# One row load of 128 partitions dealt as 120 and 8 partitions in a DMA-bound RMSNorm-and-repeat kernel

## The chip, the cores and the metric

The kernel runs on one core of one Trainium2 chip. The metric is the device time of an execution in microseconds (us). The two versions are compared by runs that alternate on the same chip.

## The reference

```python
def reference(x, gamma):                       # x: 8 x 512 x 2048 float32, gamma: 2048
    x_rep = np.repeat(x, 2, axis=1)            # each row twice
    rms = np.sqrt((x_rep ** 2).mean(axis=-1, keepdims=True) + 1e-6)
    return ((x_rep / rms) * gamma[None, None, :]).astype(np.float32)
```

33.6 MB are read and 67.1 MB are written, as the output has each row twice.

## The kernel before

The 4096 input rows are cut into 8 tiles. A tile has 128 partitions with K = 4 rows each. The SBUF tile `y` has 8 row slots for a partition: the four input rows are loaded into the upper four slots, and the results are written over the slots from below. There are three such buffers.

```python
    K = 4
    x_t = x.rearrange("b s d -> (b s) d").rearrange("(n p k) d -> n p k d", p=P, k=K)
    rows = ctx.enter_context(tc.tile_pool(name="rows", bufs=3))
    # ... other pools cut

    def load(i, parts=1):
        y = rows.tile([P, K * R, D], f32, name="y")
        step = K // parts
        for k in range(0, K, step):
            at = K * (R - 1) + k
            nc.sync.dma_start(out=y[:, at : at + step, :], in_=x_t[i, :, k : k + step, :])
        ys.append(y)

    load(0, parts=K)          # tile 0 row by row: four DMAs of 1 MB
    # ... gamma: one row from the ScalarE queue, then broadcast by GpSimd; eps by VectorE
    load(1)                   # 4 MB each
    load(2)
    for i in range(ntiles):
        for k in range(K):    # ScalarE: square with sum, sqrt; VectorE: reciprocal, x * rstd * gamma; one copy
            ...
        nc.sync.dma_start(out=out_t[i], in_=y.rearrange("p j d -> p (j d)"))   # 8 MB
        if i >= 1 and i + 2 < ntiles:
            load(i + 2)
```

Below, rows 0 to 3 are the four row loads of tile 0; the second and the third load are those of tiles 1 and 2.

Of the kernel before, what the change touches and what calls it, by code (L numbers as in the profile page):

```python
# [1 line left out]

# [4 lines left out]


@with_exitstack
def kernel(  # L10
    ctx: ExitStack,
    tc: tile.TileContext,
    x: bass.AP,
    gamma: bass.AP,
    out: bass.AP,
):
    nc = tc.nc
    P = nc.NUM_PARTITIONS
    f32 = mybir.dt.float32
    Act = mybir.ActivationFunctionType  # L20
    Alu = mybir.AluOpType

    B, S, D = x.shape
    Bo, So, Do = out.shape
    R = So // S
    assert R == 2 and D == Do and B == Bo and So == S * R
    eps = 1e-6
    inv_d = 1.0 / float(D)


    K = 4
    N = B * S
    assert N % (P * K) == 0
    ntiles = N // (P * K)
    x_t = x.rearrange("b s d -> (b s) d").rearrange("(n p k) d -> n p k d", p=P, k=K)
    out_t = out.rearrange("b s d -> (b s) d").rearrange("(n p j) d -> n p (j d)", p=P, j=K * R)

    singles = ctx.enter_context(tc.tile_pool(name="singles", bufs=1))
    rows = ctx.enter_context(tc.tile_pool(name="rows", bufs=3))
    junk = ctx.enter_context(tc.tile_pool(name="junk", bufs=1, space=bass.MemoryType.PSUM))  # L40
    small = ctx.enter_context(tc.tile_pool(name="small", bufs=8))

    ys = []

    def load(i, parts=1):


        y = rows.tile([P, K * R, D], f32, name="y")
        step = K // parts
        for k in range(0, K, step):  # L50
            at = K * (R - 1) + k
            nc.sync.dma_start(out=y[:, at : at + step, :], in_=x_t[i, :, k : k + step, :])  # L52
        ys.append(y)

    load(0, parts=K)
    gamma_b = singles.tile([P, D], f32, name="gamma_b")
    nc.scalar.dma_start(out=gamma_b[0:1, :], in_=gamma.partition_broadcast(1))
    nc.gpsimd.partition_broadcast(out_ap=gamma_b[:], in_ap=gamma_b[0:1, :])  # L58
    eps_t = singles.tile([P, 1], f32, name="eps_t")
    nc.vector.memset(eps_t, eps)  # L60
    load(1)
    load(2)

    for i in range(ntiles):
        y = ys[i]
        for k in range(K):
            xk = y[:, K * (R - 1) + k, :]
            y0, y1 = y[:, R * k, :], y[:, R * k + 1, :]
            sq = junk.tile([P, D], f32, name="sq")
            ss = small.tile([P, 1], f32, name="ss")  # L70
            nc.scalar.activation(out=sq[:], in_=xk, func=Act.Square, accum_out=ss[:])  # L71
            rms = small.tile([P, 1], f32, name="rms")
            nc.scalar.activation(out=rms[:], in_=ss[:], func=Act.Sqrt, scale=inv_d, bias=eps_t[:])  # L73
            rstd = small.tile([P, 1], f32, name="rstd")
            nc.vector.reciprocal(out=rstd[:], in_=rms[:])  # L75
            nc.vector.scalar_tensor_tensor(  # L76
                out=y0, in0=xk, scalar=rstd[:], in1=gamma_b[:],
                op0=Alu.mult, op1=Alu.mult,
            )
            if k == K - 1:  # L80
                nc.vector.tensor_copy(out=y1, in_=y0)  # L81
            else:
                nc.scalar.copy(out=y1, in_=y0)  # L83
        nc.sync.dma_start(out=out_t[i], in_=y.rearrange("p j d -> p (j d)"))  # L84
        if i >= 1 and i + 2 < ntiles:
            load(i + 2)


# [1 line left out]
_INS = ['x', 'gamma']  # L90
_OUTS = [((8, 1024, 2048), 'float32')]


# [23 lines left out]
```

## Time and profile before

| | before |
|---|---|
| time, median of 3 runs | 240.11 us (239.83 to 241.21) |
| span of the profiled run | 239.1 us |
| bytes moved, mean rate | 100.69 MB, 421 GB/s |
| VectorE, ScalarE busy | 37%, 49% |

All large DMAs are issued by SyncE and work through one queue in order: it has 100.66 of the 100.69 MB. The page's list of DMA issues gives the count, the KB of one and the median time from issue to landing:

```profile
y<-in_x_dram SPq DMA_DIRECT2D x7, 4096.0 KB, 38.8
y<-in_x_dram SPq DMA_DIRECT2D x4, 1024.0 KB, 8.0
out_dram<-y SPq DMA_DIRECT2D x8, 32.0
```

A 4 MB load takes 38.8 us to land although its data need 9.7 us (8 packets of 1.213 us on each engine). The rest is time behind other DMAs in the same queue.

DVE is VectorE, ACT is ScalarE, and SPq is SyncE issuing DMAs.

Two further readings come from the trace's records of DMA. A **landing mark** is the update of a DMA's semaphore by one of the engines; a DMA over all 16 engines has 16, as each 128-partition load of the kernel before shows. A **packet** is one partition's part of a DMA (8 KB in a row load, 32 KB in a tile's load, 64 KB in a store), with start and duration.

### The profile page before, as it was taken

What the parts mean: (1) busy time and instruction counts of PE and PEld (TensorE: products, weight loads), DVE (VectorE), ACT (ScalarE), POOL (GpSimd) and SP (SyncE); (2) the same over time, 40 slices, a digit from 0 to 9 for tenths busy, and PEclk for the clock granted to TensorE, in tenths of its full rate; (3) what the DMA queues carried; (4) which work ended last, traced back from release to release, by engine and by line L of the source; (5) the groups of instructions that cost most, each with busy time, mean ns of one, the idle gap of its engine ahead of it and who ended that gap; (6) DMA issues with size and microseconds to landing.
All of it is one profiled execution on the core that took longest, in us unless ns stands there. A gap on an engine that the chain in (4) does not pass through costs nothing.

```text
span 239.1 us, 293 instructions
## 1 busy us (share of the span) xinstructions
DVE 88.8 (37%) x73; ACT 116.3 (49%) x122; POOL 2.5 (1%) x5
## 2 busy tenths in 40 slices
DVE  0449759590000085400863016820168202591000
ACT  2998999950000299104990059800598006970000
POOL 4000000000000000000000000000000000000000
DMA  7999998989899999899898999899989899898984
GB/s 262 426 454 439 439 439 351 526 351 526 351 428 439 493 395 451 384 411 510 362 515 351 439 439 506 373 422 433 493 384 471 362 461 461 384 482 384 493 384 175
DMA packets 2741, 100.69 MB, mean 421 GB/s; under 512 B 306, under 2 KB 306, under 8 KB 306
## 3 DMA queue, kind: packets, MB, share of 16 engines
q1 hardware_dynamic: 2736, 100.66, 98.3%
q14 instruction: 3, 0.02, 0.0%
q10 hardware_dynamic: 2, 0.01, 0.0%
HBM read 33.56 MB, written 67.11 MB: 421 GB/s over the span
## 4 chain that ended last, share of the span: by engine, by line
DMA 68%; ACT 13%; DVE 8%; SPq 1%; issue 1%
DMA y<-in_x_dram 41%; DMA out_dram<-y 27%; ACT sq L71 7%; DVE y L76 6%; ACT y L83 5%; DVE y L81 2%; SPq L52 1%; ACT rms L73 1%; DVE rstd L75 0%; SPq L84 0%
## 5 line engine op out<-in xcount | busy, mean ns | idle before, releaser
L71 ACT ACTIVATE sq<-y 128x2048 f32<-128x2048 f32 x32 | 59.7, 1865 | 92.5 <-DMA y<-in_x_dram 92.5
L76 DVE SCALAR_TENSOR_TENSOR y<-y,rstd,gamma_b 128x2048 f32<-128x2048 f32 x32 | 75.3, 2352 | 1.2
L75 DVE RECIPROCAL rstd<-rms 128x1 f32<-128x1 f32 x32 | 5.1, 159 | 124.8 <-ACT rms L73 124.8
L83 ACT COPY y<-y 128x2048 f32<-128x2048 f32 x24 | 44.7, 1890 | 3.2 <-DVE y L76 3.2
L81 DVE COPY y<-y 128x2048 f32<-128x2048 f32 x8 | 9.8, 1226 | 0.3
L73 ACT ACTIVATE rms<-ss,eps_t 128x1 f32<-128x1 f32 x32 | 9.4, 293 | 0.7
L71 ACT ACTIVATION_READ_ACCUMULATOR sq<-y 128x1 f32 x32 | 6.0, 186 | 0.0
L58 POOL PARTITION_BROADCAST gamma_b<-gamma_b x1 | 2.3, 2293 | 2.1 <-DMA gamma_b<-in_gamma_dram 2.1
L71 ACT ACT_TABLE_LOAD x1 | 1.3, 1283 | 1.3 <-PEq L101 1.3
L73 ACT ACT_TABLE_LOAD x1 | 1.3, 1283 | 0.0
L60 DVE MEMSET eps_t<- 128x1 f32 x1 | 0.1, 59 | 0.8 <-PEq L101 0.8
L101 POOL MEMSET const-bfloat16-1.0<- 128x1 bf16 x1 | 0.1, 101 | 0.0
L101 POOL MEMSET const-uint8-127<- 128x1 uint8 x1 | 0.1, 101 | 0.0
L101 POOL MEMSET const-float32-0.0<- 128x1 f32 x1 | 0.1, 98 | 0.2 <-issue 0.2
L101 POOL MEMSET const-float32-1.0<- 128x1 f32 x1 | 0.1, 99 | 0.0
## 6 DMA issues: line engine op xcount, KB each, us to landing
y<-in_x_dram SPq DMA_DIRECT2D x7, 4096.0 KB, 38.8
y<-in_x_dram SPq DMA_DIRECT2D x4, 1024.0 KB, 8.0
out_dram<-y SPq DMA_DIRECT2D x8, 32.0
gamma_b<-in_gamma_dram ACTq DMA_DIRECT2D x1, 8.0 KB
```

The lines of the kernel that those rows point to most:

```text
L52: nc.sync.dma_start(out=y[:, at : at + step, :], in_=x_t[i, :, k : k + step, :])
L58: nc.gpsimd.partition_broadcast(out_ap=gamma_b[:], in_ap=gamma_b[0:1, :])
L60: nc.vector.memset(eps_t, eps)
L71: nc.scalar.activation(out=sq[:], in_=xk, func=Act.Square, accum_out=ss[:])
L73: nc.scalar.activation(out=rms[:], in_=ss[:], func=Act.Sqrt, scale=inv_d, bias=eps_t[:])
L75: nc.vector.reciprocal(out=rstd[:], in_=rms[:])
L76: nc.vector.scalar_tensor_tensor(out=y0, in0=xk, scalar=rstd[:], in1=gamma_b[:], op0=Alu.mult, op1=Alu.mult,)
L81: nc.vector.tensor_copy(out=y1, in_=y0)
L83: nc.scalar.copy(out=y1, in_=y0)
L101: nc = _bacc.Bacc("TRN2", target_bir_lowering=False, num_devices=1)
```

## The change

Row 0 of tile 0 is loaded by two DMAs, of partitions 0 to 119 and 120 to 127. If the DMA of 120 rows goes over 15 engines with 8 rows each, and that of 8 rows over eight, the intent is plain: take 8 rows off one engine and give one more to each of eight others, if that one engine is what ends late.

```diff
-            nc.sync.dma_start(out=y[:, at : at + step, :], in_=x_t[i, :, k : k + step, :])
+
+            cuts = (0, 120, P) if i == 0 and k < 1 else (0, P)
+            for p0, p1 in zip(cuts, cuts[1:]):
+                nc.sync.dma_start(out=y[p0:p1, at : at + step, :], in_=x_t[i, p0:p1, k : k + step, :])
```

All later lines of the kernel move down by three: the square is line 74, the load line 55, the store line 87.

## The prediction

The prediction numbers the 16 engines as names, since no trace numbers them: "15" is the one that the 120 rows leave out, "0 to 7" are those of the 8 rows. Before the run this deal was the author's estimate. So is rival 1: the packets of the two DMAs take longer, those of the 120 rows up to twice 309 ns, those of the 8 rows four times. No trace of the kernel before shows these factors.

> **What bounds the kernel now.** I read the page first: the slices, the queue table and the chain.
>
> ```profile
> DVE  0449759590000085400863016820168202591000
> ACT  2998999950000299104990059800598006970000
> ...
> DMA  7999998989899999899898999899989899898984
> ...
> q1 hardware_dynamic: 2736, 100.66, 98.3%
> ...
> DMA 68%; ACT 13%; DVE 8%; SPq 1%; issue 1%
> ```
>
> The DMA row is at 8 or 9 from the second slice to the last but one, while VectorE and ScalarE have whole slices of zero. All 100.66 MB go over one queue, whose packets fill 98.3% of the time of 16 DMA engines. The kernel is bound by its bytes. I checked that by a sum. The packets in the trace have three sizes with steady durations: 8 KB in 309 ns, 32 KB in 1213 ns, 64 KB in 2418 ns (medians). One engine of 16 carries 4 x 8 rows of 8 KB, 7 x 8 of 32 KB and 8 x 8 of 64 KB: 32 x 0.309 + 56 x 1.213 + 64 x 2.418 = 9.9 + 67.9 + 154.8 = 232.6 us. The first packet starts at 1.73 us, so an engine without a hitch would end at 234.3; the last packet ends at 237.66. Only some 3 us are slack or stalls.
>
> Second, the timeline of the SyncE queue and of the start, to see whether a queue ever runs dry.
>
> ```profile
> 0.72 3.20 SPq L52 DMA_DIRECT2D y<-in_x_dram  x6
> 24.12 15.65 SPq L84 DMA_DIRECT2D out_dram<-y  x2
> ...
> 5.67 1.88 ACT L71 ACTIVATE sq<-y 128x2048 f32<-128x2048 f32 x1 [3.11 <-DMA y<-in_x_dram]
> ```
>
> Six loads are issued in the first 3.9 us. ScalarE starts on row 0 of tile 0 at 5.67, when it lands, and tile 0's store is issued at 24.12. The third tile's load lands at 33.4, so the first store waits 8 to 9 us in the queue behind loads. A late first row costs compute time that is hidden. Line 71 of the kernel is the square, line 52 the load, line 84 the store.
>
> Third, the chain of waits at the end, the one place where compute comes close.
>
> ```profile
> 159.68 39.68 DMA y<-in_x_dram
> 199.36 0.02 issue
> 199.38 2.01 ACT sq L71 x2
> ...
> 212.30 2.36 DVE y L76
> 214.66 0.02 issue
> 214.68 1.23 DVE y L81
> ```
>
> The last load lands at 199.36, compute ends at 215.9, the last store is issued at 215.97. The engines leave the store before it between 216.80 and 218.69. An issue takes about 1.0 us to its first packet (issue 0.72, packet 1.73), so the quick engines wait a moment and the slow ones do not.
>
> Fourth, the landing marks. The trace has, for each 128-partition DMA, 16 marks, one per DMA engine, in order of time. Those of the first row run from 5.06 to 5.64 us; those of the last load from 197.49 to 199.36, eleven within 0.35 us and the last two at 199.32 and 199.36; those of the last store at 236.53 to 236.66 (eleven), then 236.96, 237.08, 237.27, 237.95, 237.99. So **two** engines run last, 0.04 us apart and 1.3 to 1.4 us behind the body, and the end is theirs. Linking each packet to the one that starts as it ends gives the same: the two were 0.3 us behind the median early and lost about 1.1 us more in the loads after 100 us.
>
> [...]
>
> **The change part by part.**
> - Issues: one more DMA on SyncE. Row loads take 0.38 to 0.66 us to issue there, so the second row's is about 0.45 us later (1.16 to about 1.6). The rows' data take 2.47 us each (8 x 0.309), so the queues stay ahead: hidden. No instruction of another engine is added; the order shows ScalarE waiting for one more semaphore before its first square.
> - Engine 15: 8 packets of 8 KB fewer, 8 x 0.309 = -2.47 us of work. It also starts only at the third issue, two issues later (about 0.9 us), so it runs about 1.6 us ahead.
> - Engines 0 to 7: one packet more, +0.31 us each. Engines 8 to 14: nothing. The bytes are the same: 8 x 15 + 8 = 128 rows.
> - First square: it now waits for engines 0 to 7's ninth packet, 5.67 + 0.31 = about 6.0 us. Hidden, with 8 us to spare.
> - The end: since engines are busy to the end, a shift at the start stays. [...] If the late pair is 15 and one of 8 to 14, the end stays at 237.95. If neither is 15, 0 to +0.3. Relieving one of two tied engines gains 0.04 us at most.
>
> Sum without further effects: 240.11 + 0 to 0.3 = about 240.1 to 240.4.
>
> **The rivals.**
> 1. [...] each packet up to twice as long, +2.47 us for the row; [...] 4 x 0.309 = 1.24 us in place of 0.31. Together up to 3.7 us on engines 0 to 7, which stays to the end: up to 243.8. For it: 64 KB in 2.42 us, 27 GB/s, looks like a hard limit[...]. Against it: the first row is already spread by latency (first packets of 0.47 to 1.33 us against 0.309 later), so part of a conflict hides. I give it a bit under one half, with half its full size as the likely value.
> 2. **A gain at the tail.** The two late engines lose time together, in the same loads, as if they share something. If relieving 15 relieves both, the last load lands up to 1.6 us earlier, the last store is issued earlier and the end falls to about 236.5: up to -1.4 us, 238.7. It can't be more: the body of the engines ends at 236.5. I give it one in six.
> 3. **A new wait in compute**, the first row landing later and pulling the first store late. It needs more than 8 us at the start; even rival 1 gives below 4. Nothing.
> 4. **ScalarE or VectorE as the bound**: 116.3 and 88.8 us busy of 239.1. Nothing.
>
> **Range and chances.** Weights: unchanged to +0.4 us, about 0.4; contention of +0.5 to +3.7 us, 0.42; gain of up to 1.4 us, 0.16. The runs of the kernel before already spread from 239.83 to 241.21. I put the middle at **240.5 us** and the range at 239.2 to 243.2. Faster by over 2% would need 4.8 us, more than the 3 us or so that are slack, so 0.01; slower by over 2% needs +4.8 us, more than the full contention[...]: 0.04. Within 2%: 0.95.
>
> **What the profile after would show.** Right: the DMA with 120 partitions has 15 late marks and one early, that with 8 partitions 8 late ones; the second and later rows' marks show one engine about 1.6 us ahead of the others; the first square starts near 6.0; the queue stays at 98%; the last store still has at least one engine 1.3 us behind the body. Rival 1: the first row's packets longer than 309 ns after the first ones, the square starting at 7 us or later, and every later landing late by as much. Rival 2: the last store's 16 marks within 0.7 us. The prediction is wrong if 120 partitions go to fewer than 15 engines (8 engines with 15 rows each would cost 7 x 0.309 = 2.2 us at once)[...].

## More of the kernel before

The view by windows gives the stretch, its length, the busy us (and instructions) of VectorE, ScalarE and GpSimd, and the granted clock. The last two numbers are the share of the 16 DMA engines' time and GB/s, counted from the packets that start in the stretch, so a share can be over 1.

```profile
3.00:13.00 10.00, 3.56 (x4) 6.82 (x8) 1.85 (x1) 1.00 1.05 442
5.00:7.00 2.00, 0.00 (x0) 1.33 (x1) 0.00 (x0) 1.00 1.04 438
```

The four row loads run at full rate from 3 us on, as fast as later stretches (442 GB/s here, 439 from 13 to 33 us).

## The result, and the profile after

| | before | after |
|---|---|---|
| median | 240.17 us (239.83 to 241.21, 4 runs) | 243.35 us (242.31 to 243.69, 4 runs) |
| ratio | | 1.0118, 95% interval 1.0073 to 1.0163 |

A ratio here is the mean time of one kernel's fast runs over the mean of the other's of the same rounds, so it is not quite the ratio of the medians. The changed kernel is **1.2% slower**, some 2.8 us. By the 2% line this still counts as the same.

Lines of the page of the kernel after, the slices of DMA and the queue:

```profile
DMA  7999999898989998999898999899989898988984
...
q1 hardware_dynamic: 2743, 100.66, 97.9%
```

These hardly tell the two apart. The engines count as busy all the time; the bytes are the same; seven packets are new, which are semaphore marks (the queue has 311 packets of 4 bytes in place of 304). The loss is visible only where busy engines move less. The same windows as before, of the kernel after:

```profile
3.00:13.00 10.00, 0.00 (x0) 3.87 (x4) 1.96 (x1) 1.00 1.00 303
5.00:7.00 2.00, 0.00 (x0) 0.00 (x0) 0.00 (x0) 1.00 1.13 209
```

From 5 to 7 us the engines were as busy as before and moved 209 GB/s in place of 438: half. Nearly every 8 KB packet that started between 3.5 and 6.5 us took about 520 to 650 ns, where before it took 309.

SyncE's queue and ScalarE's start, from the timeline of the kernel after:

```profile
0.72 4.93 SPq L55 DMA_DIRECT2D y<-in_x_dram  x7
28.85 14.98 SPq L87 DMA_DIRECT2D out_dram<-y  x2
...
9.10 1.28 ACT L74 ACT_TABLE_LOAD   x1 [9.10 <-DMA y<-in_x_dram]
10.40 1.88 ACT L74 ACTIVATE sq<-y 128x2048 f32<-128x2048 f32 x1
```

The seven issues took 4.93 us in place of 3.20 for six. The first square starts at 10.40 in place of 5.67, for two reasons. The row landed 3.4 us later. And the compiler put the wait for the second semaphore on the table load just ahead of the square, so that 1.28 us of table load, which before had run in ScalarE's idle time at 1.27, now followed the wait. The first store was issued at 28.85. The third load's first engine finished at 34.90, so all this was hidden.

The end of the chain of waits, after:

```profile
162.80 39.26 DMA y<-in_x_dram
202.06 0.02 issue
202.08 2.01 ACT sq L74 x2
...
217.38 1.23 DVE y L84
```

This end of the chain is the same as before, 2.7 us later: the last load landed at 202.06 in place of 199.36. The last landing marks of each DMA show where the loss came in:

| last mark of | before | after | difference |
|---|---|---|---|
| row 0 (after: its 120 rows, its 8 rows) | 5.64 | 8.38, 9.03 | +2.7, +3.4 |
| row 1 | 8.12 | 11.22 | +3.1 |
| row 3 | 13.08 | 16.18 | +3.1 |
| second load | 22.80 | 25.91 | +3.1 |
| third load | 33.41 | 35.62 | +2.2 |
| last load | 199.36 | 202.06 | +2.7 |
| last store | 237.99 | 240.80 | +2.8 |

About 3.1 us came in while row 0 was loaded, and 0.9 us of it was given back in the third load. The difference then grew again, from 2.2 to 2.8 us. I draw nothing from that: two profiles of the kernel before already differ by 0.8 us in the last store (237.99 and 237.16, table below).

### The profile page after: what moved, and what is told of

Same layout as the page of the kernel before. It is cut to its first block, busy times and chain, and to the rows that moved or that the text cites. A ratio compares the mean times of both kernels' runs of the same rounds, so it can differ in the third digit from the quotient of the medians.

```text
span 241.8 us, 295 instructions
## 1 busy us (share of the span) xinstructions
DVE 88.8 (37%) x73; ACT 116.2 (48%) x122; POOL 2.5 (1%) x5
## 4 chain that ended last, share of the span: by engine, by line
DMA 62%; ACT 17%; DVE 10%; issue 1%; SPq 0%; DVEq 0%; ACTq 0%
DMA y<-in_x_dram 36%; DMA out_dram<-y 26%; ACT sq L74 9%; DVE y L79 8%; ACT y L86 7%; DVE y L84 2%; ACT rms L76 1%; ACT L76 1%; DVE rstd L78 0%; SPq L55 0%; ACT L74 0%; SPq L87 0%; DVEq L79 0%; ACTq L74 0%
```

## The experiments

**Theory P: partitions.** The partitions that a DMA writes decide how long its packets take. So far it has the change behind it: with row 0 as 120 and 8 partitions, nearly every 8 KB packet from 3.5 to 6.5 us took 520 to 650 ns, and from 5 to 7 us the rate was 209 GB/s; with all 128 in one DMA they took 309 ns, at 438 GB/s. For the runs to come P makes estimates from the 309 ns: 618 (twice) for the halves of 64, less for 112 partitions, 1.24 us (four times) for 8 adjacent partitions, and 309 for 8 stepped ones. The factors are the author's estimate, and no trace shows what lies behind them: the traces have no addresses.

The rivals: **H**, the new order of reading collides in HBM; **K**, the engine left out or a number of engines other than 16 costs; **D**, one more DMA and its wait cost by themselves; **S**, any shape other than 128 is slow; **N**, the loss belongs to the start alone.

Twelve runs were made, one of them the kernel before once more. They came in three batches of four on three chips, so marks of different batches come from different chips. "Row 3", "2nd" and "3rd load" and "last store" are the last landing marks of each DMA in us; two profiles of the kernel before stand first. The ratio is to the kernel before in the same rounds.

| kernel | row 3 | 2nd load | 3rd load | last store | ratio (95% interval) |
|---|---|---|---|---|---|
| before | 13.08 | 22.80 | 33.41 | 237.99 | |
| before, again | 12.87 | 22.60 | 33.41 | 237.16 | 1.0020 (0.9968 to 1.0072) |
| the change | 16.18 | 25.91 | 35.62 | 240.80 | 1.0118 (1.0073 to 1.0163) |
| change, other rows of the input | 16.17 | 25.88 | 35.59 | 240.78 | 1.0120 (1.0099 to 1.0140) |
| row 0 as 64 + 64 | 15.54 | 25.25 | 34.96 | 239.09 | 1.0075 (1.0038 to 1.0113) |
| row 0 as 112 + 16 | 14.44 | 24.16 | 33.87 | 238.13 | 0.9994 (0.9963 to 1.0024) |
| row 0 as two column halves | 14.17 | 23.89 | 33.90 | 237.98 | 1.0013 (0.9974 to 1.0053) |
| change on all four rows | 25.76 | 35.24 | 44.96 | 248.49 | 1.0433 (1.0403 to 1.0462) |
| 8 more rows, adjacent, behind row 0 | 14.03 | 23.75 | 33.46 | 238.42 | 1.0030 (1.0001 to 1.0059) |
| 8 more rows, stepped, behind row 0 | 14.67 | 24.39 | 34.64 | 239.35 | 1.0071 (1.0048 to 1.0093) |
| 8 more rows, adjacent, behind row 3 | 13.83 | 24.09 | 33.80 | 238.20 | 1.0027 (0.9993 to 1.0061) |
| 8 more rows, stepped, behind row 3 | 12.83 | 22.86 | 33.62 | 238.64 | 1.0055 (1.0019 to 1.0090) |
| change, row 1 from ScalarE's queue | 16.71 | 26.43 | 36.12 | 241.19 | 1.0167 (1.0138 to 1.0196) |
| store of tile 3 as 64 + 64 | 12.87 | 22.59 | 33.36 | 257.68 | one look: 260.49 us |

All results were correct but that of the first experiment.

### Is it the HBM side?

The two DMAs read rows 40 KB apart in place of 32 KB.

```diff
+    x_5 = x.rearrange("b s d -> (b s) d")[0 : 5 * P, :].rearrange("(p f) d -> p f d", f=5)
-                nc.sync.dma_start(out=y[p0:p1, at : at + step, :], in_=x_t[i, p0:p1, k : k + step, :])
+                src = x_t[i, p0:p1, k : k + step, :]
+                if len(cuts) == 3:
+                    src = x_5[p0:p1, 0:1, :]
+                nc.sync.dma_start(out=y[p0:p1, at : at + step, :], in_=src)
```

> The same deal of 120 and 8 partitions, but the two DMAs read other rows of the input, 40 KB apart in place of 32 KB (tile 0's row 0 is wrong on purpose). Theory P [...]: nothing changes, packets of the first row near 600 ns between 3.5 and 6.5 us, last mark of the 8-row DMA near 9.0 us, time +2 to +3.5 us over the kernel before. Rival H (rows that lie a power of two apart in HBM collide): packets at 309 ns, first row landed by 6.2 us, time within +0.5 us of before.

The marks in the table agree with the change's within 0.03 us and the ratio is 1.0120 against 1.0118. H falls: with another distance between the rows in HBM, and the same deal over partitions and engines, the loss is the same.

### Two halves of 64

```diff
-            cuts = (0, 120, P) if i == 0 and k < 1 else (0, P)
+            cuts = (0, 64, P) if i == 0 and k < 1 else (0, P)
```

> Row 0 as 64 and 64 partitions: both DMAs go over 16 engines, none is left out, no small DMA. P: [...] packets near 618 ns, the row takes 4.94 us in place of 2.47, second half's last mark near 8.1 us, time +2.0 to +2.8 us. Rival K (the loss comes from the left-out engine or from a number of engines other than 16) and rival D (from the small DMA of 8 rows): packets at 309 ns, row landed by 5.9 us, time within +0.4 us of before.

Both DMAs have 16 marks, so no engine is left out and none is small. The window from 5 to 7 us of this run:

```profile
5.00:7.00 2.00, 0.00 (x0) 0.00 (x0) 0.00 (x0) 1.00 1.02 217
```

Again half the rate. Row 3 is 2.46 us late, and P's estimate from twice the packet time was 4.94 - 2.47 = 2.47. The time, +1.8 us by the ratio, is a little below what was expected, as here too the third load gave back 0.9 us. K falls as the main cause: there is no left-out engine here, and 2.5 of the 3.1 us are lost all the same.

### 112 and 16: a loss between

```diff
+            cuts = (0, 112, P) if i == 0 and k < 1 else (0, P)
```

> Row 0 as 112 and 16 partitions: both over 16 engines, none left out. P[...] the 112 rows cost less than the halves of 64 did[...]. Last mark of row 3 between 14.0 and 15.2 us (13.1 before, 15.5 with halves, 16.2 with the change), time +0.7 to +2.0 us. Rival S (any number of partitions other than 128 runs at half rate[...]): row 3 lands at 15.5 us or later, as with halves.

Row 3 landed at 14.44, in the expected window. Packets of the 112 rows took about 390 to 460 ns between 3.5 and 5 us, between 309 and 618, and those around the 16 rows 620 to 910. S falls, since another shape than 128 runs here well above half rate.

The packets don't fall into fast ones of 309 ns and slow ones of 618: no packet that started between 3.7 and 5 us took less than 350 ns, so all engines slowed together. The change shows the same: row 0 had landed by 5.64 us before, and the first late mark of the 120 rows came at 7.04. By time, the kernel of 112 and 16 is level with before, which is below the expected +0.7: of 1.36 us in the marks, 0.9 came back in the third load.

### One DMA more, with all 128 partitions

Row 0 as two DMAs of 128 partitions, with half of the columns each.

```diff
+            cuts = (0, D // 2, D) if i == 0 and k < 1 else (0, D)
+            for c0, c1 in zip(cuts, cuts[1:]):
+                src, dst = x_t[i, :, k : k + step, c0:c1], y[:, at : at + step, c0:c1]
+                nc.sync.dma_start(out=dst, in_=src)
```

> Row 0 as two DMAs that both have all 128 partitions, with 1024 of the 2048 columns each: one DMA and one wait more, as in the change[...]. P: packets at full rate (about 155 ns for 4 KB), first row landed by 6.0 us, time within +0.4 us of before. D (one more DMA and its wait cost by themselves): time +1 us or more.

By time D falls: 1.0013, with 1 inside the interval. But the marks show something that P had not foreseen. The two halves landed by 5.40, earlier than row 0 before, and then the engines were idle for some 2 engine-us (idle time summed over the engines) between 4.7 and 5.5 us, as row 1's packets had not arrived. Row 1 was issued at 1.64. Row 3 was up to 1.1 us late on six engines. In the last store nothing of it is to be seen (237.98).

### 8 more rows: adjacent against stepped partitions

The kernel before, with one more DMA of 8 rows behind row 0, into a part of the tile that is overwritten later; once into partitions 120 to 127 (adjacent), once into 0, 4, 8 to 28 (stepped, `y[0:32:4, 3:4, :]`).

```diff
+            if i == 0 and k == 0:
+                nc.sync.dma_start(out=y[120:128, 3:4, :], in_=x_t[i, 0:8, 0:1, :])
```

> The kernel before, with one more DMA of 8 rows, 64 KB, behind row 0, into partitions 120 to 127 of a part of the tile that is overwritten later. P: [...] packets of about 1.0 to 1.24 us on engines 0 to 7; later marks shift by 0.9 to 1.5 us, time +0.9 to +1.5 us. D (a small DMA costs by itself): the same shift as the run with stepped partitions.

> As the run before this, but the 8 rows go to partitions 0, 4, 8 to 28. P: [...] packets of 309 ns, later marks of 8 engines shift by 0.31 us, time +0.0 to +0.5 us. D: the same shift as with adjacent partitions, 0.9 us or more.

Of the adjacent form, the 8 rows' marks came at 6.32 to 6.77, the first of them 1.3 us behind the first of row 0. Sixteen packets around it took 0.9 to 1.15 us, twice as many as it has: about one for each engine. The stepped form's marks came at 5.30 to 5.58, the first 0.3 us behind the first of row 0: packets at full speed. Both forms read the same 8 rows of HBM, in the same place of the queue; only the partitions that they write differ. So the slow packets come from which partitions are written, as P says, and H has no part in it. That all engines are slowed goes beyond P, which expected it of the eight with the 8 rows. In the time P is wrong: the stepped form is the slower one, 1.0071 against 1.0030. D isn't right either, which expected the same shift of both. The stepped run's engines stood idle for some 3.5 engine-us around 5 us, at least one of them for a full microsecond, and from then on one engine landed last, by 0.9 us and more (row 3: 13.79 for the last but one, 14.67 for the last). So a second effect exists, **Q**: near the start, a DMA behind another one or two reaches the engines late, and a short one ahead of it lets the queue run dry (some 3.5 engine-us idle here, 2 with column halves).

### The same 8 rows, behind row 3

```diff
-            if i == 0 and k == 0:
+            if i == 0 and k == 3:
```

> The extra DMA of 8 rows to partitions 120 to 127, behind row 3. P: [...] its packets about 1 us, the next load's marks +0.9 us over the stepped form's +0.3 and so near 23.6 us at the last (22.7 before). Time +0.2 to +1.2 us, since the third load lost 1 us by itself in before and not always in others. Rival (the cost at the start was the dry queue): same as the stepped form within 0.3 us in the marks.

> The extra DMA of 8 rows to partitions 0, 4 to 28, now behind row 3 in place of row 0, when the queues are many DMAs deep. Theory P with Q (its cost of 1.7 us at the start came from queues that ran dry near 5 us, 3.8 engine-us lost[...]): no engine idle, marks of later loads +0.31 us on 8 engines, time within +0.5 us of before. Rival D (a DMA over fewer than 16 engines costs about 1 us wherever it stands): +1 us or more.

The stepped form has the other partitions, as above. No engine ran dry in either. In the next load's last mark the adjacent form is 1.23 us behind the stepped one, 24.09 against 22.86; the estimate was 0.93 (1.24 - 0.31). The packets show how. With the adjacent rows, the first 32 KB packet of the second load took 1.8 to 2.4 us on each of the 16 engines; with the stepped rows it took 1.21 on all. The 8 rows' own packets, expected at about 1 us, took 0.8 at most. So 8 rows in adjacent partitions cost some 0.9 to 1.2 us of all engines, at the start as well as behind row 3. By what path engines without one of the 8 rows are held up, no run here shows. The stepped form has left no delay in the marks of the second load, as P with Q expects. Its time is a miss: +1.3 us where +0.5 at most was expected. In its last store three engines ended at 238.11 to 238.64, with the rest at 237.35 or before. Delays of that kind came and went, between the two profiles of the kernel before too; I can't tell whether this DMA had a part in them.

### All four rows

```diff
-            cuts = (0, 120, P) if i == 0 and k < 1 else (0, P)
+            cuts = (0, 120, P) if i == 0 else (0, P)
```

> The change on all four rows of tile 0 in place of one. P: each row costs what the first did, about 3 us in the marks (3.1 us measured for one), so the last row of tile 0 lands near 25 us (13.1 before, 16.2 with one row) and the time is +11 to +13 us over before. Rival N (the loss belongs to the start, where queues are empty and latency is long): the later rows cost little, time below +5 us.

The window from 3 to 13 us of this run:

```profile
3.00:13.00 10.00, 0.00 (x0) 4.03 (x4) 1.86 (x1) 1.00 1.03 214
```

Ten microseconds at half the rate. Row 3 is 12.7 us late, 3.2 for each row, and the time is +10.4 us by the ratio, just under the expected 11. N falls. Here one engine did run ahead: the second load's first mark came at 27.80, the next at 33.59. It gained nothing for the end, since tiles are computed and stored when their last engine has landed (in the kernel before, the second load's last mark is at 22.80 us and the square of its first row starts at 22.82).

### The left-out engine

In the change's trace, by linking packets, one engine began its first row load at about 5.7 us, and no mark of row 1 came before 10.50. So the left-out engine had no head start. Row 1 was therefore issued from ScalarE's queue:

```diff
+                q = nc.scalar if i == 0 and k == 1 else nc.sync
+                q.dma_start(out=y[p0:p1, at : at + step, :], in_=x_t[i, p0:p1, k : k + step, :])
```

> The change, with row 1's load issued by ScalarE's queue at the start in place of SyncE's. It asks why engine 15, left out of row 0, did not begin before 5.7 us. Theory Q (the third DMA of one queue reaches the engines some 3 us after its issue, so whatever queue position the left-out engine waits for is late): engine 15 begins by 3 us and its marks run 1.5 us or more ahead of the others; [...] row 3 lands at 15.5 to 16.5 us and the time is +2 to +3.2 us. Rival [...]: it begins after 5 us again.

Row 1's first mark came at 6.75, the others of it from 10.65 on. In the second load one engine landed at 23.71 and the rest from 25.79, so it was 2.1 us ahead. Q is right: what held the engine was the position of its first DMA in SyncE's queue. The lead was worth nothing again; row 3 and the time came out slightly above what was expected (16.71 against 16.5 at most, +4.0 us against 3.2), with rows 0 and 1 in mixed order.

### Reading from SBUF

The store of tile 3 in two halves, one look.

```diff
+        cuts = (0, 64, P) if i == 3 else (0, P)
+        for p0, p1 in zip(cuts, cuts[1:]):
+            nc.sync.dma_start(out=out_t[i, p0:p1], in_=y[p0:p1].rearrange("p j d -> p (j d)"))
```

> The store of tile 3 as 64 and 64 partitions, all else as before. P[...]: the two halves take twice the 19.35 us of a store, time +17 to +20 us. If reading isn't bound: within 1 us.

The last mark is 19.7 us later than before. The 64 KB packets of this store took about 5.12 us in place of 2.42, a little over twice. The time of the one look is 20.3 us over the median of before, just above what was expected. Windows of this run, then of the kernel before:

```profile
101.00:130.00 29.00, 11.11 (x9) 14.25 (x15) 0.00 (x0) 1.00 1.07 307
130.00:159.00 29.00, 0.00 (x0) 0.00 (x0) 0.00 (x0) 1.00 0.93 268
```

```profile
101.00:130.00 29.00, 11.11 (x9) 14.25 (x15) 0.00 (x0) 1.00 1.00 432
130.00:159.00 29.00, 11.11 (x9) 14.25 (x15) 0.00 (x0) 1.00 1.00 433
```

The engines are about as busy as before, at 307 and 268 GB/s in place of 432 and 433. A store in halves pays about what a load in halves does: 19.7 us for 8 MB, 2.46 for 1 MB. No run with other addresses in HBM was made for stores, so that the partitions are the cause is likely for them, not shown.

### The kernel before, once more

> The kernel before once more, unchanged, for the scatter between runs and to see whether the stretched packets of the third load (near 29 to 32 us, about 1 us lost) in the profile of before come again. Both theories: ratio 1.000 within 0.004; the stretch may or may not come again.

The ratio is 1.0020. The slow stretch in the third load came again: the load took 10.8 us, against 10.6 in the first profile. The last section returns to it.

## Why the prediction was right or wrong

- **The bound** was right: the time is set by DMA, and the chain ends in the same way before and after.
- **"Within 2%"** was right. The point, 240.5 us, was 2.9 us too low. The median of 243.35 lies just over the upper end of 243.2; the ratio times the 240.11 us of before gives 242.9, inside by 0.3 us. That the range reaches so far is owed to rival 1; on which side of its end the result falls is luck.
- **The engines** were right: the DMA of 120 partitions has one early mark (1.30) and 15 late ones (7.04 to 8.38), that of 8 partitions one early (1.68) and 8 late ones (8.10 to 9.03). The counts are those of the estimate; which engines they are, no trace shows.
- **Rival 1 was what happened.** The step that failed is its weight and size, a term of the sum that was set too low: "half its full size as the likely value". Of the full 3.7 us (2.47 for the row, 1.24 for the 8 rows), 3.1 arrived in the marks, where half would be 1.9. The measured parts are 2.46 us for a row at half rate, from the halves, and 0.95 to 1.2 for 8 adjacent rows. The argument against it, that latency hides a conflict, was worth a few tenths at most, and nothing in the halves. Rival 1 was right in that the packets slow down, and not in whose: it laid its full sum on engines 0 to 7, and all 15 engines of the 120 rows were slow (first late mark at 7.04). What lies behind the slow packets, no run shows. For the larger value the prediction had one steady rate in hand, 26.5 to 27.1 GB/s in packets of all three sizes, which it called a likely hard limit; that such a limit makes the full doubling likely was its estimate, not shown before the run.
- **"Sum without further effects"**, 0 to 0.3 us, failed for the same reason. It counted packets for each engine and took each packet's 309 ns as fixed; they are the time of a packet of the DMA of 128 partitions, and nearly all of the change's between 3.5 and 6.5 us took 520 to 650.
- **"Engine 15 ... runs about 1.6 us ahead"** failed. It counted 0.9 us for a start at the third issue; the engine started at about 5.7 us. In the change's second load no engine was ahead by more than 0.06 us. In the run with other rows it was 0.7.
- **"First square ... about 6.0 us"** failed: 10.40. It missed 3.1 us of slow packets and the 1.28 us of table load behind the wait. The step that this is hidden was right.
- **Rival 2** did not happen: the last store's marks after have 14 engines within 0.27 us, then 239.90 and 240.80. Which engines are late was not settled.
- **"A shift at the start stays"** held but for 0.9 us, for which the prediction has no step.

## What to carry to other kernels

If a transfer between HBM and SBUF has to be cut, try it along columns before partitions: here two column halves cost nothing in time (ratio 1.0013), halves of 64 partitions 2.5 us in the marks of a row and 19.7 us in those of a store. Check the GB/s of the stretch and not the DMA engines' busy share, which stayed at full (1.13) while the rate fell to half. Fewer bytes for one engine gained nothing here: in the change it began at about 5.7 us and had no lead, and where it ran 2.1 us ahead, tiles still waited for their last engine. A shift in a queue that doesn't run dry was paid once here and kept to the end but for 0.9 us (3.1 us at row 3, 2.2 at the third load, 2.8 at the last store), so count it at its place and expect most of it in the total.

## What stays open

- Why engines without one of the 8 rows are slowed. With 8 adjacent rows behind row 3, the next packet of each of the 16 engines took 1.8 to 2.4 us in place of 1.21.
- Why near the start the third DMA of the queue reached the engines only some 3 to 4 us after its issue: row 1's packets were missing at 4.7 to 5.5 us with column halves (issued at 1.64), and the left-out engine began at about 5.7 (issued at 1.56).
- The stretch of the third load. In both profiles of the kernel before, and in the runs of the divided store and of the stepped rows behind row 3, its packets that started near 29 and 30.5 us took up to 1.7 and 2.4 us in place of 1.21, and the load took 10.6 to 10.8 us. In all eight runs with slow packets ahead of it (the change, on one row and on four, other rows, 64 + 64, 112 + 16, adjacent rows twice, row 1 from ScalarE) it took 9.7 us and had no such stretch. The column halves and the stepped rows behind row 0 lay between, at 10.0 and 10.3. It does not follow the issue of the first store, which came at 22.19 in the stepped and 22.36 us in the adjacent run behind row 3. I have no explanation for it. It is why 0.9 us of the change's delay came back.
